# Weight sums on VectorE, squares on ScalarE, tiles of 512 bytes, seven products for four more chunks, and transposes of the identity at the start

## The chip, the cores and the metric

One core of a Trainium2 chip runs the whole program in one launch. The metric is the device time of one execution in microseconds (us). The kernel before takes 1533.81 us, the median of three runs (1532.96 to 1535.28).

## What is computed

Two layers of an encoder over 512 tokens of 1024 features, in float32. Each layer has three token mixers that share one input projection, gates, an output projection, a layer norm, and then the part that the change is about, a squared-ReLU network:

```python
ff = jnp.square(jax.nn.relu(x @ w_up[layer])) @ w_down[layer]      # (512,1024) @ (1024,4096), then @ (4096,1024)
x = layer_norm(DEEPNORM_ALPHA * x + ff, ln2_g[layer], ln2_b[layer])
```

## The kernel before, in words

**Products.** Every float32 operand is split into a high and a low part. ScalarE (ACT) writes the high part (L182 for weights, tiles `whi`), VectorE (DVE) subtracts it from the operand (L183, `wlo`), and `mm3` (L153 to L155) makes one product out of three matmuls of TensorE (PE): high by high, high by low, low by high. A weight chunk is 128 x 1024 numbers, 512 KB. `Stream` brings the chunks in a planned order: SyncE (SP) issues a load into one of two `raw` tiles, the chunk is split, and at most eight split chunks are held (five in one pool, three in another). One more chunk is split each time one is taken.

**The squared-ReLU network.** It runs in four quarters `q` of 8 chunks of 128 hidden features. For each chunk m, 24 matmuls make x @ w_up in a PSUM bank (`psu`). Then `hidden(m)` takes it over: ACT applies Relu into tile `f` (L910), DVE squares it in place (L911), ACT and DVE split it (`split_psum`, L231 and L232) into `hh` and `hl`. In quarters 0 to 2 DVE also makes sums of pairs of blocks (L918, L921). The tile `f` has one buffer. A pair of chunks (m even, m odd) shares it, so the Relu of the next pair waits until the last `hl` of this pair is written.

**Seven products.** In quarters 0 to 2 the 8 chunks of `w_down` are multiplied by the class `Fast`: two by two blocks, seven products instead of eight. Each product takes two split chunks (halves 0 and 1) and 24 matmuls into two `psd` banks, and DVE adds each bank to x (L259). The operands of the products are quarters of the weights and their differences: `operand(i, half)` gives seven operands for each half, four of which are a difference (L796, 128x1024, GpSimd = POOL). One load comes late: quarter 2 goes into the `y` tile (i = 5) only after i = 4 has been split from it, and the difference i = 6 needs it. All three `Fast` runs of a layer use the same raw tiles (`braw`). In quarter 3 the last 8 chunks go through `token_major` plainly: 8 chunks x 8 banks x 3 = 192 matmuls.

**Order.** Tile, the layer that places the instructions, orders each engine's queue. An engine takes its instructions strictly in that order, so an instruction that waits holds up all behind it. At the first quarter of a layer (q = 0) the first four chunks are done in two passes over the tokens, because the layer norm before it is still finishing.

**Tiles.** `LINE` = 16 numbers pads small tiles to 64 bytes, and the tile `edge` on the right side makes up for the rest.

Of the kernel before, what the change touches and what calls it, by code (L numbers as in the profile page):

```python
# [11 lines left out]
F32 = mybir.dt.float32  # L12
# [5 lines left out]
P = 128  # L18
L = 2
# [18 lines left out]
C_WID = 1280  # L38
LINE = 16


class Split:


    def __init__(self, hi, lo):
        self.hi, self.lo = hi, lo
# [82 lines left out]
def encoder(ctx: ExitStack, tc: tile.TileContext, x, x_t, w_qkv, w_c, w_gate, b_gate, qn, kn, rpb,  # L129
            w_ba, w_bb, w_bc, w_out, ln1_g, ln1_b, w_up, w_down, w_fast, ln2_g, ln2_b,  # L130
            mask_a, rope_a, rope_b, out):
# [5 lines left out]
    edge = ctx.enter_context(tc.tile_pool(name="edge", bufs=1, side="right"))  # L137
    edge.tile([P, LINE // 2], F32, name="edge")
    psum = ctx.enter_context(tc.tile_pool(name="psum", bufs=8, space=bass.MemoryType.PSUM))
# [9 lines left out]
    nhalf = const.tile([P, 16], F32, name="nhalf")  # L149
    nc.vector.memset(nhalf, -0.5)  # L150

    def mm3(ps, lhs, rhs, start, stop, again=False):
# [145 lines left out]
    def attention(l, keep, qk, open_heads):  # L298
# [72 lines left out]
        def norm_rotate(tb):  # L371
# [7 lines left out]
            yield 1  # L379
            ss = pool.tile([P, 2, LINE], F32, tag="ss", name="ss", bufs=2)[:, :, :10]  # L380
            nc.vector.tensor_reduce(ss[:, 0], sq, axis=AX.X, op=ALU.add)
# [128 lines left out]
        def scores(name, h, qb):  # L510
            ks, qs = pairs[name, h // 2]
            q, k = qs[h % 2], ks[h % 2]
            k0, k1 = keys_of(name, qb)
            n = (k1 - k0) * P
            ps = bank("pss")[:, :n]
            nc.tensor.matmul(ps, q[:, qb * P:(qb + 1) * P], k.hi[:, k0 * P:k1 * P], start=True, stop=False)
            nc.tensor.matmul(ps, q[:, qb * P:(qb + 1) * P], k.lo[:, k0 * P:k1 * P], start=False, stop=True)
            p = pool.tile([P, S], F32, tag="p", name="p", bufs=4)[:, :n]
            st = pool.tile([P, LINE], F32, tag="stat", name="stat", bufs=4)
# [132 lines left out]
        pool = open_heads()  # L652
        hb = keep.tile([P, 4 * KB], F32, tag="hb", name="hb")[:, :3 * KB]
        nc.sync.dma_start(hb, b_gate[l])
# [110 lines left out]
    class Fast:  # L765
# [8 lines left out]

        def __init__(self, pools, src):
            self.pools, self.src = pools, src
            self.b = {}

        def load(self, quarter, half, into):
            t = self.pools["mlp"].tile([P, 1024], F32, tag=f"b{into}{half}", name="braw")  # L780
            nc.sync.dma_start(t, self.src[quarter, half])
            self.b[into, half] = t

        def operand(self, i, half):

            if i == 0 and half == 0:
                for quarter in (0, 1, 3):
                    for h in range(2):
                        self.load(quarter, h, quarter)
            if i == 5:  # L790
                self.load(2, half, 1)
            b11, b12, b22 = (self.b[k, half] for k in (0, 1, 3))
            dst, a, b = ((b11, None, None), (b11, b12, b11), (b11, b22, b11), (b22, None, None),
                         (b12, b22, b12), (b12, None, None), (b11, b12, b11))[i]
            if a is not None:
                nc.gpsimd.tensor_tensor(dst, a, b, op=ALU.subtract)  # L796
            return dst

        def items(self):
            return [lambda i=i, half=half: self.operand(i, half) for i in range(7) for half in range(2)]  # L800

        def run(self, hid, done):
            ps = {}
            for a, _, name, (i, n) in self.ORDER:
                w = [stream.take(2) for _ in range(2)]
                new = name not in ps
                if new:
                    ps[name] = [bank("psd") for _ in range(2)]
                for t in range(2):
                    for j in range(4):  # L810
                        lhs = hid[j].map(lambda h: h[:, a - 1, t * P:(t + 1) * P])
                        mm3(ps[name][t], lhs, w[j // 2][:, j % 2], new and j == 0, j == 3, True)
                    done(2 * (1 - i) + t, n, ps[name][t])
# [23 lines left out]
    for l in range(L):  # L837
        with ExitStack() as left:
# [59 lines left out]
            for q in range(4):  # L898
                hid, sums = [], []

                def hidden(m, ps):
# [22 lines left out]
                for m0 in range(0, 8, 4):  # L924
                    cut = [(0, 2), (2, 4)] if q == 0 and m0 == 0 else [(0, 4)]
                    ws, ps = [], []
                    for a, b in cut:
                        for i in range(4):
# [8 lines left out]
                            elif i in (0, 2):  # L937
                                late.popleft()()

                if q < 3:  # L940
                    def add(tb, n, ps):
                        add_stats(mlp, xs[tb], ps, n, 1.0 if (tb, n) in started else ALPHA, None)
                        started.add((tb, n))

                    fast[q].run(sums, add)
                    continue
# [17 lines left out]
                stream.burst = 2  # L964
                whole = [h.map(lambda t: t[:, 2 * i:2 * i + 2].rearrange("p a n -> p (a n)")) for h in sums for i in range(2)]
                token_major(whole, 8, half_done, done, between)
                stream.burst = 1
# [56 lines left out]

def _quarters(w):

    w = w[:, :24 * P].reshape(L, 3, 2, 2, 2, P, 2, 512).transpose(0, 1, 4, 6, 2, 5, 3, 7)
    return w.reshape(L, 3, 4, 2, P, 1024)

# [52 lines left out]
```

## Time and profile before

| | |
|---|---|
| median of three runs | 1533.81 us |
| the profiled execution, all of it | 1538.57 us |
| its span, first to last instruction | 1536.8 us |
| PE busy | 1501.1 us, 98% |
| DVE busy | 1096.1 us, 71% |
| ACT busy | 688.0 us, 45% |
| POOL busy | 311.6 us, 20% |
| mean granted clock of TensorE | 0.991 |

Busy times are sums over the whole span; matmuls are pipelined, so a busy PE is not a PE at its peak. PE runs from 6.97 us almost to the end: where PE stands still, and at which clock it runs, is what the time is made of. [...]

### The profile page before, as it was taken

How to read it: one execution, taken by the hardware profiler on the slowest of the kernel's cores; microseconds unless marked ns; L12 is line 12 of the kernel's file. 1: busy time of each engine (PE TensorE's matmuls, PEld its weight loads, DVE VectorE, ACT ScalarE, POOL GpSimd, SP SyncE). 2: the span in 40 equal slices, each digit the busy share in tenths (PEclk: the TensorE clock that was granted, in tenths of full speed). 3: DMA queues.
4: the chain of work that ended last, by engine and by line, in shares of the span. 5: the costliest groups of instructions: out<-in, count | busy, mean ns of one | idle time of the engine just before them, and what ended most of it. 6: DMA issues, size and time to landing. Idle time of an engine off the chain costs nothing.

```text
span 1536.8 us, 19258 instructions
## 1 busy us (share of the span) xinstructions
PE 1501.1 (98%) x7256; PEld 1255.7 (82%) x7256; DVE 1096.1 (71%) x1722; ACT 688.0 (45%) x1096; POOL 311.6 (20%) x238
## 2 busy tenths in 40 slices
PE   7999999999998999999999999999999989999997
PEld 6888888888896888888888888888888968888886
DVE  4677977745588797964666787876447888979636
ACT  4565656533134343433236556565332343535320
POOL 0112212311142222210101141233111413222001
PEclk9999999999998999999999999999999999999999
DMA  6222321143242415042331323112441342340411
GB/s 218 84 79 70 112 68 53 58 164 118 75 178 81 139 56 164 1 131 85 114 129 56 99 77 110 55 55 76 160 133 56 152 137 83 91 129 28 138 55 55
DMA packets 43438, 150.63 MB, mean 98 GB/s; under 512 B 5073, under 2 KB 5713, under 8 KB 43345
## 3 DMA queue, kind: packets, MB, share of 16 engines
q1 hardware_dynamic: 43344, 149.40, 30.8%
q8 instruction: 57, 0.93, 0.2%
q14 instruction: 37, 0.30, 0.1%
HBM read 145.19 MB, written 4.19 MB: 97 GB/s over the span
## 4 chain that ended last, share of the span: by engine, by line
PE 88%; DVE 7%; ACT 2%; issue 1%; DMA 1%; POOL 0%; SPq 0%; POOLq 0%; DVEq 0%; ACTq 0%
PE psd L153 8%; PE psd L154 8%; PE psd L155 8%; PE psu L154 6%; PE psu L153 6%; PE psu L155 6%; PE psg L155 6%; PE psg L154 6%; PE psg L153 6%; PE psp L547 3%; PE psq L153 2%; PE psq L155 2%; PE psq L154 2%; DVE wlo L183 2%; PE psb L155 2%; PE psb L153 2%
## 5 line engine op out<-in xcount | busy, mean ns | idle before, releaser
L183 DVE TENSOR_TENSOR wlo<-raw,whi 128x1024 fp32r<-128x1024 f32 (+1 forms) x198 | 247.9, 1253 | 204.2 <-ACT whi L182 201.9
L182 ACT ACTIVATE whi<-raw 128x1024 fp32r<-128x1024 f32 (+1 forms) x198 | 207.7, 1051 | 268.7 <-DMA raw<-in_w_up 110.6
L153 PE MATMUL psu<-xTh,whi 128*128 128x512 f32 (+1 forms) x576 | 210.8, 366 | 0.0
L154 PE MATMUL psu<-xTl,whi 128*128 128x512 f32 (+1 forms) x576 | 210.7, 366 | 0.0
L155 PE MATMUL psu<-xTh,wlo 128*128 128x512 f32 (+1 forms) x576 | 210.4, 365 | 0.0
L153 PE MATMUL psd<-whi,hh 128*128 128x512 f32 x464 | 183.2, 395 | 14.8 <-ACT hh L231 14.8
L796 POOL TENSOR_TENSOR braw<-braw 128x1024 f32<-128x1024 f32 x48 | 130.1, 2713 | 332.7 <-DVE wlo L183 169.2
L154 PE MATMUL psd<-wlo,hh 128*128 128x512 f32 x464 | 182.3, 393 | 0.0
L155 PE MATMUL psd<-whi,hl 128*128 128x512 f32 x464 | 182.2, 393 | 0.0
L153 PE MATMUL psg<-xTh,whi 128*128 128x512 f32 x384 | 156.7, 408 | 0.0
L155 PE MATMUL psg<-xTh,wlo 128*128 128x512 f32 x384 | 151.6, 395 | 0.0
L154 PE MATMUL psg<-xTl,whi 128*128 128x512 f32 x384 | 151.5, 395 | 0.0
L532 POOL TENSOR_SCALAR p<-p,stat 128x512 f32<-128x512 f32 x96 | 70.4, 734 | 361.5 <-DVE stat L531 247.1
L183 DVE TENSOR_TENSOR wlo<-braw,whi 128x1024 fp32r<-128x1024 f32 x84 | 126.7, 1508 | 18.3 <-ACT whi L182 16.7
L231 ACT ACTIVATE hh<-f 128x768 fp32r<-128x768 f32 (+2 forms) x88 | 60.8, 691 | 144.8 <-DVE f L918 79.4
L153 PEld LDWEIGHTS psu<-xTh,whi 128*128 128x128 f32 x576 | 108.6, 189 | 17.5
L154 PEld LDWEIGHTS psu<-xTl,whi 128*128 128x128 f32 x576 | 108.6, 189 | 17.5
L155 PEld LDWEIGHTS psu<-xTh,wlo 128*128 128x128 f32 x576 | 108.6, 189 | 17.5
L153 PEld LDWEIGHTS psd<-whi,hh 128*128 128x128 f32 x464 | 88.3, 190 | 34.8 <-ACT hh L231 16.5
L182 ACT ACTIVATE whi<-braw 128x1024 fp32r<-128x1024 f32 x84 | 87.9, 1051 | 47.9 <-DMA braw<-in_w_fast 25.3
L155 PEld LDWEIGHTS psd<-whi,hl 128*128 128x128 f32 x464 | 88.1, 190 | 18.9 <-DVE hl L232 0.5
L154 PEld LDWEIGHTS psd<-wlo,hh 128*128 128x128 f32 x464 | 88.3, 190 | 18.3
(121 smaller groups left out, 2991.3 us busy)
## 6 DMA issues: line engine op xcount, KB each, us to landing
raw<-in_w_up SPq DMA_DIRECT2D x64, 512.0 KB, 3.7
raw<-in_w_gate SPq DMA_DIRECT2D x48, 512.0 KB, 3.6
braw<-in_w_fast SPq DMA_DIRECT2D x48, 512.0 KB, 3.7
raw<-in_w_qkv SPq DMA_DIRECT2D x22, 512.0 KB, 3.6
raw<-in_w_out SPq DMA_DIRECT2D x16, 512.0 KB, 3.5
raw<-in_w_down SPq DMA_DIRECT2D x16, 512.0 KB, 3.5
raw<-in_w_c SPq DMA_DIRECT2D x12, 512.0 KB, 3.6
bias<-in_rpb SPq DMA_DIRECT2D x8, 640.0 KB, 4.0
```

Source lines behind the costliest of these rows:

```text
L153: nc.tensor.matmul(ps, lhs.hi, rhs.hi, start=start, stop=False, skip_group_check=again)
L154: nc.tensor.matmul(ps, lhs.hi, rhs.lo, start=False, stop=False, skip_group_check=again)
L155: nc.tensor.matmul(ps, lhs.lo, rhs.hi, start=False, stop=stop, skip_group_check=again)
L182: nc.scalar.activation(hi[:, s], raw[:, s], AF.Copy)
L183: nc.vector.tensor_tensor(lo[:, s], raw[:, s], f32(hi[:, s]), op=ALU.subtract)
L231: nc.scalar.activation(dst.hi, ps, AF.Copy)
L532: (nc.vector if name == "c" else nc.gpsimd).tensor_scalar(p, p, st[:, 3:4], 1.0, op0=ALU.mult, op1=ALU.mult)
L547: nc.tensor.transpose(ps[:, j * P:(j + 1) * P], p[:, j * P:(j + 1) * P], ident)
L796: nc.gpsimd.tensor_tensor(dst, a, b, op=ALU.subtract)
```

## The change

Five things change. (1) The differences of weights (L796) go from POOL to DVE. (2) The square (L911) goes from DVE to ACT (`AF.Square`). (3) All tiles are padded so that they start at multiples of 512 bytes: `ROW` = 128 numbers in place of `LINE` in most small tiles, a tile `pad`, another `edge`. (4) In quarter 3, chunks 0 to 3 go through `Fast` with one half (`tiles` = 1): seven products of 12 matmuls, in place of 4 chunks x 24; chunks 4 to 7 go through `token_major` as before. For this `Fast`, quarter 2 of the weights has a tile of its own (`y1`) and the first difference another (`x1`). (5) 24 transposes of the identity into an unused bank stand ahead of PE's first matmul.

```diff
+    const.tile([P, 3 * ROW // 4], F32, name="pad")
     ident = const.tile([P, P], F32, name="ident")
     make_identity(nc, ident)
...
+    idle = bank("idle")
+    for _ in range(24):
+        nc.tensor.transpose(idle[:, :P], ident, ident)
...
         def operand(self, i, half):
+            one = self.tiles == 1
             if i == 0 and half == 0:
...
+                if one:
+                    self.b["y1"], self.b["x1"] = self.room("y1"), self.room("x1")
+                    nc.sync.dma_start(self.b["y1"], self.src[2, 0])
+            if i == 5 and not one:
+                self.load(2, f"y{half}")
+            x, y, w = (self.b[f"{name}{half}"] for name in "xyw")
+            t1, last, b21 = (self.b["x1"], self.b["x1"], self.b["y1"]) if one else (x, x, y)
+            dst, a, b = ((x, None, None), (t1, y, x), (x, w, t1), (w, None, None),
+                         (y, w, y), (b21, None, None), (last, b21, x))[i]
             if a is not None:
-                nc.gpsimd.tensor_tensor(dst, a, b, op=ALU.subtract)
+                nc.vector.tensor_tensor(dst, a, b, op=ALU.subtract)
...
-                w = [stream.take(2) for _ in range(2)]
+                w = [stream.take(2) for _ in range(self.tiles)]
...
-                    for j in range(4):
+                    for j in range(2 * self.tiles):
...
-            fast = [Fast(pools, w_fast[l, q]) for q in range(3)]
+            fast = [Fast(pools, w_fast[l, q], 2) for q in range(3)] + [Fast(pools, w_last[l], 1)]
             plan = []
             for q in range(4):
                 plan += [w_up[l, q * 8 + m] for m in range(8)]
-                plan += fast[q].items() if q < 3 else [w_down[l, m] for m in range(8)]
+                plan += fast[q].items()
+            plan += [w_down[l, m] for m in range(4)]
...
                     nc.scalar.activation(r, ps.rearrange("p (a n) -> p a n", a=2), AF.Relu)
-                    nc.vector.tensor_tensor(r, r, r, op=ALU.mult)
-                    if q == 3:
+                    nc.scalar.activation(r, r, AF.Square)
+                    if q == 3 and m > 3:
...
-                token_major(whole, 8, half_done, done, between)
+                token_major(whole, 4, half_done, done, between)
```

On DVE in quarter 0 of layer 0, before, from the last `wlo` of the up-projection on (`f` 128x512 is a square, `f` 128x256 a sum of blocks, `wlo<-braw` the split of a `Fast` operand):

```order
L183 TENSOR_TENSOR wlo<-raw,whi 128x1024
L911 TENSOR_TENSOR f<-f 128x512
L921 TENSOR_TENSOR f<-f 128x256
L183 TENSOR_TENSOR wlo<-braw,whi 128x1024
L232 TENSOR_TENSOR hl<-f,hh 128x256
L183 TENSOR_TENSOR wlo<-braw,whi 128x1024
L911 TENSOR_TENSOR f<-f 128x512
L918 TENSOR_TENSOR f<-f 128x256
L921 TENSOR_TENSOR f<-f 128x256 x2
L183 TENSOR_TENSOR wlo<-braw,whi 128x1024
L232 TENSOR_TENSOR hl<-f,hh 128x768 x2
L183 TENSOR_TENSOR wlo<-braw,whi 128x1024
```

The same place now:

```order
L190 TENSOR_TENSOR wlo<-raw,whi 128x1024
L190 TENSOR_TENSOR wlo<-braw,whi 128x1024
L239 TENSOR_TENSOR hl<-f,hh 128x256
L937 TENSOR_TENSOR f<-f 128x256
L811 TENSOR_TENSOR braw<-braw 128x1024
L190 TENSOR_TENSOR wlo<-braw,whi 128x1024
L934 TENSOR_TENSOR f<-f 128x256
L811 TENSOR_TENSOR braw<-braw 128x1024
L937 TENSOR_TENSOR f<-f 128x256
L239 TENSOR_TENSOR hl<-f,hh 128x768
L937 TENSOR_TENSOR f<-f 128x256
L190 TENSOR_TENSOR wlo<-braw,whi 128x1024 x2
```

The squares have left DVE's queue here, and the differences (`braw<-braw`) stand between the splits and the sums of blocks; six of them stand ahead of the `hl` on which the first product of this quarter waits.

On DVE a little later, when the first products of that quarter run (`x<-x,psd` takes a finished bank), before:

```order
L259 SCALAR_TENSOR_TENSOR x<-x,psd 128x512
L183 TENSOR_TENSOR wlo<-braw,whi 128x1024
L259 SCALAR_TENSOR_TENSOR x<-x,psd 128x512
L183 TENSOR_TENSOR wlo<-braw,whi 128x1024
L259 SCALAR_TENSOR_TENSOR x<-x,psd 128x512
```

And now:

```order
L266 SCALAR_TENSOR_TENSOR x<-x,psd 128x512
L190 TENSOR_TENSOR wlo<-braw,whi 128x1024
L266 SCALAR_TENSOR_TENSOR x<-x,psd 128x512
L811 TENSOR_TENSOR braw<-braw 128x1024
L190 TENSOR_TENSOR wlo<-braw,whi 128x1024
L266 SCALAR_TENSOR_TENSOR x<-x,psd 128x512
L811 TENSOR_TENSOR braw<-braw 128x1024
L266 SCALAR_TENSOR_TENSOR x<-x,psd 128x512
```

The two differences i = 6 of the run, which need the late load of quarter 2, now stand in DVE's queue between the takings of the banks.

On ACT in quarter 0 of layer 0, now, from the last up-projection chunk on (`f<-psu` is the Relu; `f<-f` is the square, which was on DVE; before, the rows are the same without `f<-f`):

```order
L189 ACTIVATE whi<-raw 128x1024
L926 ACTIVATE f<-psu 128x512
L189 ACTIVATE whi<-braw 128x1024
L927 ACTIVATE f<-f 128x512
L238 ACTIVATE hh<-f 128x256
L189 ACTIVATE whi<-braw 128x1024
L926 ACTIVATE f<-psu 128x512
L927 ACTIVATE f<-f 128x512
```

The square now follows the Relu on the same engine, and the split follows the square.

## Rows read from the trace of the kernel before

**Rows 1.** The page, part 1: busy us, share of the span, instructions.

```profile
PE 1501.1 (98%) x7256; PEld 1255.7 (82%) x7256; DVE 1096.1 (71%) x1722; ACT 688.0 (45%) x1096; POOL 311.6 (20%) x238
```

**Rows 2.** Waits of PE: who waited for whom, us in total, times, longest.

```profile
PE psd L153 <- ACT hh L231: 14.8, 3, 7.4
...
PE psp L547 <- POOL p L532: 4.6, 2, 2.5
```

**Rows 3.** Windows of PE: stretch, length, busy (instructions), granted clock, DMA share, GB/s.

```profile
520.00:560.00 40.00, 40.00 (x179) 1.00 0.12 37
565.00:600.00 35.00, 35.00 (x156) 1.00 0.56 172
...
54.90:59.00 4.10, 4.10 (x15) 0.58 0.27 109
475.20:485.30 10.10, 5.69 (x13) 0.50 0.35 105
1236.40:1243.10 6.70, 3.83 (x9) 0.50 0.36 94
...
6.90:17.40 10.50, 9.28 (x19) 1.00 0.77 294
```

**Rows 4.** Timeline of PE at quarter 0: start us, us, what [idle before].

```profile
470.56 0.39 PE L154 MATMUL psd<-wlo,hh 128*128 128x512 f32 x1
...
472.15 0.39 PE L155 MATMUL psd<-whi,hl 128*128 128x512 f32 x1
479.61 0.80 PE L153 MATMUL psd<-whi,hh 128*128 128x512 f32 x1 [7.07 <-ACT hh L231]
...
1239.27 0.80 PE L153 MATMUL psd<-whi,hh 128*128 128x512 f32 x1 [7.36 <-ACT hh L231]
```

**Rows 5.** Timeline of DVE in quarter 0 of layer 0.

```profile
444.01 2.71 DVE L183 TENSOR_TENSOR wlo<-braw,whi 128x1024 fp32r<-128x1024 f32 x1 [0.65 <-ACT whi L182]
...
461.20 3.49 DVE L911 TENSOR_TENSOR f<-f 128x512 f32<-128x512 f32 x2
...
464.95 0.41 DVE L918 TENSOR_TENSOR f<-f 128x256 f32<-128x256 f32 x1
...
468.41 0.95 DVE L232 TENSOR_TENSOR hl<-f,hh 128x768 fp32r<-128x768 f32 x1
470.09 0.69 DVE L911 TENSOR_TENSOR f<-f 128x512 f32<-128x512 f32 x1 [0.72 <-ACT f L910]
...
479.59 0.43 DVE L232 TENSOR_TENSOR hl<-f,hh 128x256 fp32r<-128x256 f32 x1
```

**Rows 6.** Groups by line and shape: busy us, mean ns of one, idle before.

```profile
L183 DVE TENSOR_TENSOR wlo<-raw,whi 128x1024 fp32r<-128x1024 f32 x11 | 13.4, 1221 | 10.2 <-ACT whi L182 10.1
L183 DVE TENSOR_TENSOR wlo<-braw,whi 128x1024 fp32r<-128x1024 f32 x84 | 126.7, 1508 | 18.3 <-ACT whi L182 16.7 <-DMA raw<-in_w_up 0.5 <-PE psu L154 0.5
L231 ACT ACTIVATE hh<-f 128x512 fp32r<-128x512 f32 x16 | 10.1, 633 | 19.9 <-DVE f L911 19.9
L376 ACT ACTIVATE sq<-rw 128x640 f32<-128x640 f32 x8 | 5.9, 740 | 0.3
```

**Rows 7.** Window of quarter 0, layer 0: PE, PEld, DVE, ACT, POOL busy (instructions), clock, DMA.

```profile
439.40:470.30 30.90, 30.90 (x174) 27.18 (x173) 29.24 (x25) 11.74 (x16) 16.74 (x6) 1.00 0.25 99
```

**Rows 8.** Timeline: the identity on POOL, PE's first operands, transposes at the slow clock.

```profile
1.00 0.29 POOL masks.py:199 TENSOR_SCALAR_AFFINE_SELECT ident<-ident 128x128 f32<-128x128 f32 x1
...
11.30 0.79 PE L153 MATMUL psq<-whi,xTh 128*128 128x512 f32 x1 [1.11 <-ACT xTh L825]
...
813.52 1.11 PE L547 MATMUL psp<-ident,p 128*128 128x128 f32 x4 [2.51 <-POOL p L532]
814.28 0.78 PE L154 MATMUL psg<-xTl,whi 128*128 128x512 f32 x1
```

**Rows 9.** The late load: POOL's waits for it, and its time from issue to landing.

```profile
POOL braw L796 <- DMA braw<-in_w_fast: 162.8, 11, 25.8
...
braw<-in_w_fast SPq DMA_DIRECT2D x48, 512.0 KB, 3.7
```

More of the change, by code (lines that the diff above doesn't have):

```diff
@@ L39 @@
 LINE = 16
+ROW = 128
 class Split:
@@ L137, in encoder @@
     edge = ctx.enter_context(tc.tile_pool(name="edge", bufs=1, side="right"))
-    edge.tile([P, LINE // 2], F32, name="edge")
+    edge.tile([P, ROW - LINE // 2], F32, name="edge")
     psum = ctx.enter_context(tc.tile_pool(name="psum", bufs=8, space=bass.MemoryType.PSUM))
@@ L145, in f32 @@
         return ap.bitcast(F32)
+    const.tile([P, 3 * ROW // 4], F32, name="pad")
     ident = const.tile([P, P], F32, name="ident")
     make_identity(nc, ident)
-    nhalf = const.tile([P, 16], F32, name="nhalf")
+    nhalf = const.tile([P, ROW], F32, name="nhalf")[:, :16]
     nc.vector.memset(nhalf, -0.5)
+    idle = bank("idle")
+    for _ in range(24):
+        nc.tensor.transpose(idle[:, :P], ident, ident)
     def mm3(ps, lhs, rhs, start, stop, again=False):
@@ L379, in norm_rotate @@
             yield 1
-            ss = pool.tile([P, 2, LINE], F32, tag="ss", name="ss", bufs=2)[:, :, :10]
+            ss = pool.tile([P, 2, ROW // 2], F32, tag="ss", name="ss", bufs=2)[:, :, :10]
             nc.vector.tensor_reduce(ss[:, 0], sq, axis=AX.X, op=ALU.add)
@@ L518, in scores @@
             p = pool.tile([P, S], F32, tag="p", name="p", bufs=4)[:, :n]
-            st = pool.tile([P, LINE], F32, tag="stat", name="stat", bufs=4)
+            st = pool.tile([P, ROW], F32, tag="stat", name="stat", bufs=4)
             if name == "b":
@@ L652, in attention @@
         pool = open_heads()
-        hb = keep.tile([P, 4 * KB], F32, tag="hb", name="hb")[:, :3 * KB]
+        hb = keep.tile([P, ROW], F32, tag="hb", name="hb")[:, :3 * KB]
         nc.sync.dma_start(hb, b_gate[l])
@@ L773, in encoder, with __init__, room @@
                  (6, 4, "x", (1, 1)), (3, 5, "y", (0, 0)), (2, 6, "x", (1, 0)))
-        def __init__(self, pools, src):
-            self.pools, self.src = pools, src
+        def __init__(self, pools, src, tiles):
+            self.pools, self.src, self.tiles = pools, src, tiles
             self.b = {}
[L779 to L782, printed above, removed]
+        def room(self, name):
+            return self.pools["mlp"].tile([P, 1024], F32, tag=f"b{name}", name="braw")
@@ L784, in operand, with load @@
+        def load(self, quarter, name):
+            self.b[name] = t = self.room(name)
+            nc.sync.dma_start(t, self.src[quarter, int(name[1])])
         def operand(self, i, half):
+            one = self.tiles == 1
             if i == 0 and half == 0:
[L787 to L792, printed above, removed]
@@ L793, in operand @@
-            dst, a, b = ((b11, None, None), (b11, b12, b11), (b11, b22, b11), (b22, None, None),
-                         (b12, b22, b12), (b12, None, None), (b11, b12, b11))[i]
+                for name, quarter in (("x", 0), ("y", 1), ("w", 3)):
+                    for h in range(self.tiles):
+                        self.load(quarter, f"{name}{h}")
+                if one:
+                    self.b["y1"], self.b["x1"] = self.room("y1"), self.room("x1")
+                    nc.sync.dma_start(self.b["y1"], self.src[2, 0])
@@ L797, in operand @@
             return dst
         def items(self):
-            return [lambda i=i, half=half: self.operand(i, half) for i in range(7) for half in range(2)]
+            return [lambda i=i, half=half: self.operand(i, half) for i in range(7) for half in range(self.tiles)]
         def run(self, hid, done):
@@ L938, in encoder, with add @@
                                 late.popleft()()
+                def add(tb, n, ps):
+                    add_stats(mlp, xs[tb], ps, n, 1.0 if (tb, n) in started else ALPHA, None)
+                    started.add((tb, n))
+                fast[q].run(sums, add)
                 if q < 3:
[L941 to L945, printed above, removed]
                     continue
@@ L964, in encoder @@
                 stream.burst = 2
-                whole = [h.map(lambda t: t[:, 2 * i:2 * i + 2].rearrange("p a n -> p (a n)")) for h in sums for i in range(2)]
-                token_major(whole, 8, half_done, done, between)
+                whole = [h.map(lambda t: t[:, 2 * i:2 * i + 2].rearrange("p a n -> p (a n)")) for h in sums[2:] for i in range(2)]
+                token_major(whole, 4, half_done, done, between)
                 stream.burst = 1
@@ L1022, in _by_rows, with _quarters @@
     return w.reshape(k // P // per, per, P, n).transpose(0, 2, 1, 3).reshape(-1, P, 1024)
[L1025 to L1028 removed]
+def _quarters(w, groups, tiles):
+    w = w.reshape(L, groups, tiles, 2, 2, P, 2, 512).transpose(0, 1, 4, 6, 2, 5, 3, 7)
+    return w.reshape(L, groups, 4, tiles, P, 1024)
 def _swap(g):
```

9 lines of the change are left out of this document (5 added, 4 removed).

## The prediction

> **What bounds the kernel now.** I read the busy times first, then PE's own waits, then its clock by stretch, and only then the engines that PE waits for. PE is busy 98% of the span [rows 1], and what PE waits for adds up to little: 14.8 us for `hh` and 4.6 us for `p` [rows 2], beside its start. Where nothing waits, its matmuls stand 0.227 us apart: eight of them from 470.56 to 472.15 us, 1.59 us over seven steps [rows 4]. The long stretches of up-projection (520 to 560 us) and of seven products (565 to 600 us) run at that pace, 4.5 matmuls a microsecond in both [rows 3], and nearly all else does. So the time is the number of matmuls by 0.227 us, plus the places where PE stands or runs at the slow clock. Work on DVE, ACT and POOL counts only where it makes PE stand.
>
> There are two such places of weight, and they are the same place of the program in either layer: the first product of quarter 0. In layer 0 PE makes nine matmuls of it, then stands 7.07 us until 479.61 us for the split of chunk 6; in layer 1 it stands 7.36 us until 1239.27 us [rows 4]. [...] The two places together cost 7.07 + 2.6 + 7.36 + 1.8 = 18.8 us; with the third, small wait in [rows 2] (14.8 - 14.4 = 0.4 us) it is 19.2 us.
>
> Why does PE stand there? DVE is busy 29.24 of the 30.9 us ahead of the stop, ACT only 11.74 [rows 7]. Six of DVE's rows there, from 444.01 to 461.20 us (the first and the last stand in [rows 5]), are far longer than the same work elsewhere: two weight splits, a sum of blocks, and a pair each of sums, of 768-wide splits and of squares take 19.12 us together. Clean, a weight split takes 1.22 us [rows 6], a sum 0.41, a 768-wide split 0.95, a square 0.69 [rows 5], and the six would take 2.44 + 0.41 + 0.82 + 1.90 + 1.38 = 6.95 us. POOL makes six differences at the same time (16.74 us busy [rows 7]): 12.2 us go to the two engines holding each other up.
>
> **The change, part by part.**
>
> *Fewer matmuls.* In quarter 3, 4 chunks x 24 = 96 matmuls become 7 x 12 = 84. Two layers: 24 fewer, 24 x 0.227 = **5.4 us**, all on PE. The price is three more weight splits a layer, 1.22 us each on DVE [rows 6] and about as much on ACT, and four differences. Under the seven short products (84 x 0.227 = 19 us) DVE takes 14 banks over, at 0.69 us for 512 columns [rows 5], and makes four splits: 14.5 us, it fits. Their operands are split during the up-projection, and no late load stands in this run, since quarter 2 has its own tile. I take nothing for it; were the cover gone, DVE would lag by a microsecond or so a layer.
>
> *Differences to DVE, squares to ACT.* A difference does not occur on DVE. The nearest rows are the split with the same shape: 1.22 us clean, 1.51 us in the mean of those with POOL often beside them [rows 6]. POOL now has nothing to do in these stretches, so I take 1.22. A square of a 128x512 tile does not occur on ACT: 0.63 us for a copy of that size, 0.74 us for a square of 640 columns [rows 6]; I take 0.65. ACT gets 64 of them, 42 us, in stretches where it is busy under half the time [rows 7]: hidden. For DVE's queue up to the `hl` of chunk 6, which ended at 480.02 us [rows 5]: the 12.2 us of holding up go, seven squares go (7 x 0.69 = 4.8), six differences come (7.3). That is 9.7 us less, so that `hl` is there at 470.3 us. PE wants it with its tenth matmul of the product, at 472.4 us, so the stop is gone with 2 us to spare; in layer 1, where the stop is 0.3 us longer, the same sum leaves 1.7 us. What is late next is chunk 7, whose rows the second product wants 5.4 us later; Relu, square, sum, split high and low (0.63 + 0.65 + 0.41 + 0.9, an estimate for 768 columns on ACT, + 0.95) are 3.5 us behind its bank, so it fits. Gain taken: **19.2 us**. Bounds: 0 (the stops stay) and 19.2.
>
> *Transposes of the identity.* The identity is ready at 1.29 us [rows 8]. Four transposes at the slow clock take 814.28 - 813.52 = 0.76 us [rows 8], about 0.2 each, so 24 end near 6.3 us, ahead of PE's first operands, which come after 6.90 us [rows 3]: no cost. At its start PE runs 19 matmuls in 9.28 us of busy time [rows 3], 0.43 us apart like the stretches at 0.50, though the clock column reads 1.00 there. Were the clock up by then, at most 19 x 0.2 = 3.8 us were to be had. Against that: the operands come piecemeal, and PE still stands before 11.30 us for `xTh` [rows 8]; a stop of 2.5 us for `p` is followed by a stretch with a mean clock of 0.58 [rows 2, 3]. Bounds 0 and 3.8; I take **1 us**, nearer the lower end for that reason.
> [...] No run here shows PE with transposes alone. [...]
>
> *Tiles of 512 bytes.* No row shows a tile that starts otherwise. The matmul's pace is the same with a moving operand in one piece of 2 KB (weights, 565 to 600 us) and in four pieces of 512 bytes (`xTh`, 520 to 560 us) [rows 3]; if crossing a boundary cost something, four pieces would cost more. I take 0. [...]
>
> **Sum.** 5.4 + 19.2 + 1 = 25.6 us. Against the profiled execution's own 1538.57 us that gives 1513.0. That execution lies 4.8 us above the median of 1533.81; the difference may be of the kind that goes (slow clock behind the stops) or of another, so I place the result between 1513.0 and 1508.2: **1510 us**.
>
> **Rivals.**
> *The start address does set the pace.* [...] For it: the pace is the one thing that bounds the whole program. Against it: the equal pace of the two kinds of operand above.
> [...]
>
> *The stop shrinks but stays.* The spare 2 us are gone if the six differences and eight splits cost 0.15 us more each, or if the chain over the single `f` buffer, which goes from ACT to DVE and back twice a pair, waits at a hop more. [...]
>
> *The stops stay whole*, because the order on ACT decides and not DVE's load: only 5.4 us and the start are gained, 1527 us. Against it: ACT is busy 11.74 of 30.9 us [rows 7].
>
> *Slower: DVE waits for the late load.* The differences i = 6 now stand in DVE's queue between the takings of the banks (see the order above). They need quarter 2, whose load is issued only after the split of i = 4 and takes 3.7 us to land; on POOL the same differences waited 162.8 us in all, up to 25.8 us at a time [rows 9]. A DVE that waits there takes no bank and splits nothing. A product takes 5.4 us and its bank is written again two products later, so PE feels the wait once it is over about 4 us. From a stop of 4.4 us in each of the six runs the gain of 25.6 us is used up; with a wait of a load's whole 3.7 us beyond the slack, and ten matmuls at the slow clock behind it (2 us), it is 6 x 5.7 = 34 us: 1544 us. Against it: by then the splits of i = 4 are two products ahead of PE, and the wait I count at DVE's head is about 2 us.
>
> **How the numbers follow.** Forecast (1510): 0.66. Stop shrinks (1520): 0.14. Stops stay (1527): 0.08. Slower (1540 and more): 0.06. Pace rises (1425 to 1450): 0.06. The range of 1500 to 1524 us holds the first two with the bounds of the start (0 to 3.8) and of the 4.8 us, and some room below for a slightly higher pace in the attention part; it leaves out 0.20. Faster by over 0.2% (which is about what a measurement of this kernel can tell) means under 1530.7 us: 0.66 + 0.14 + 0.06 and most of the 0.08, 0.92. Within 0.2%: 0.03, the weakest form of the stops that stay or a short wait for the load. Slower: 0.05.
>
> **What would show it.** In the profile after: PE with no wait for `hh` over 1 us near 472 and 1230 us and no stretch at 0.50 there; DVE's splits and sums near 1.22 and 0.42 us in the quarters; POOL idle in them; 7256 - 24 + 24 = 7256 matmuls, the first 24 transposes; the pace still 0.227 us. I would be wrong if the pace changes, if PE waits for `psd` banks or for `wlo` inside the products (DVE at the head of its queue waiting for a load), or if the stop at quarter 0 only moves to the next chunk.

## The result, and the profile after

The changed kernel takes 1507.31 us (median; 1506.78 to 1509.10), the kernel before, run beside it, 1534.55 us: ratio 0.9823, 95% interval 0.9805 to 0.984, so 27 us or 1.8% faster. The forecast was 1510 us, with a range of 1500 to 1524. The profiled execution took 1506.91 us, against 1538.57 us before. The two traces stand 31.7 us apart, the medians 27: the profiled execution of before was one of its longer ones, that of after was not.

The page of the changed kernel, parts 1 and 4 (busy us, share of the span, instructions; then the shares of the chain that ended last), answers [rows 1]:

```profile
PE 1488.2 (99%) x7256; PEld 1250.8 (83%) x7256; DVE 1059.8 (70%) x1768; ACT 738.5 (49%) x1170; POOL 181.9 (12%) x190
...
PE 95%; DVE 2%; DMA 1%; ACT 1%; issue 1%; POOL 0%; SPq 0%; POOLq 0%; DVEq 0%; ACTq 0%
```

PE has as many instructions as before (24 matmuls fewer, 24 transposes more) and is busy 12.9 us less. POOL's work fell from 311.6 to 181.9 us. DVE took over 56 differences (68.0 us, below) and gave 64 squares away (48 us at 0.75 before), 20 us more by that sum, and is busy 36 us *less*. What PE still waits for, against [rows 2] (who waited for whom, us in total, times, longest):

```profile
PE psp L554 <- POOL p L539: 4.3, 2, 2.4
PE psq L160 <- ACT xTh L840: 2.0, 1, 2.0
PE idle L157 <- POOL ident masks.py:199: 1.3, 1, 1.3
```

The waits for `hh` are gone, all three. The wait for `p` stands as it was. The groups of DVE and ACT by line and shape (busy us, mean ns of one | idle before) answer [rows 6]:

```profile
L190 DVE TENSOR_TENSOR wlo<-braw,whi 128x1024 fp32r<-128x1024 f32 x98 | 119.5, 1223 | 71.9 <-ACT whi L189 71.7
L811 DVE TENSOR_TENSOR braw<-braw 128x1024 f32<-128x1024 f32 x56 | 68.0, 1219 | 8.7 <-DMA braw<-in_w_fast 4.2 <-issue 2.3 <-DMA braw<-in_w_last 2.3
L937 DVE TENSOR_TENSOR f<-f 128x256 f32<-128x256 f32 x84 | 35.1, 422 | 3.3 <-ACT f L927 2.4
L927 ACT ACTIVATE f<-f 128x512 f32<-128x512 f32 x64 | 40.3, 633 | 1.8
```

A difference on DVE takes 1.22 us and a square on ACT 0.63 us. The splits of `braw` fell from 1.51 to 1.22 us in the mean. DVE stood only 6.5 us in the whole run for the loads of its differences. PE at quarter 0 of layer 0, and the split that it stood for before (PE's and DVE's timelines), answer [rows 4] and [rows 5]:

```profile
464.95 0.42 DVE L239 TENSOR_TENSOR hl<-f,hh 128x256 fp32r<-128x256 f32 x1
...
468.46 0.39 PE L162 MATMUL psd<-whi,hl 128*128 128x512 f32 x1
468.69 0.39 PE L160 MATMUL psd<-whi,hh 128*128 128x512 f32 x1
468.92 0.39 PE L161 MATMUL psd<-wlo,hh 128*128 128x512 f32 x1
```

The matmul of 468.69 us is the one that began at 479.61 us before, behind a stop of 7.07 us. Now nothing stands ahead of it, and the split is over 3.3 us before it. Windows of PE (length, busy (instructions), granted clock, DMA share, GB/s) answer [rows 3]:

```profile
520.00:560.00 40.00, 40.00 (x178) 1.00 0.18 51
565.00:600.00 35.00, 35.00 (x156) 1.00 0.52 165
440.00:480.00 40.00, 40.00 (x197) 1.00 0.26 86
11.60:14.90 3.30, 3.26 (x8) 0.50 0.83 325
52.50:55.90 3.40, 3.40 (x11) 0.50 0.51 154
796.60:800.00 3.40, 3.12 (x10) 0.50 0.56 161
```

The two long stretches run at the old pace (156 matmuls in 35 us, as before). Quarter 0 now runs through at 1.00. Slow stretches (granted clock 0.50) are left behind the stop at the start and behind the two stops for `p`. In such a stretch of before two neighbours of one product stand 0.43 us apart:

```profile
480.20 0.63 PE L154 MATMUL psd<-wlo,hh 128*128 128x512 f32 x1
480.63 0.63 PE L155 MATMUL psd<-whi,hl 128*128 128x512 f32 x1
```

From 480.20 to 484.89 us eleven steps take 4.69 us, 0.427 each, where 0.227 is the pace at 1.00.

Where the trace's 31.7 us come from can be read by pairing the same matmul in both traces:

| the same matmul | before, us | after, us | lead | gained in the stretch |
|---|---|---|---|---|
| project, first layer, early | 17.42 | 15.80 | 1.6 | 1.6: the start |
| gate, behind the stop for `p` | 58.77 | 56.85 | 1.9 | 0.3 |
| first of the output projection | 379.08 | 375.38 | 3.7 | 1.8: attention, little by little |
| quarter 0, behind the slow stretch | 485.32 | 471.63 | 13.7 | 10.0: stop and slow clock |
| last of quarter 3, layer 0 | 728.0 | 711.45 | 16.55 | 2.7 for 12 matmuls, 0.15 |
| attention of layer 1, late | 1128.33 | 1109.99 | 18.35 | 1.8: little by little |
| quarter 0, layer 1 | 1243.22 | 1215.31 | 27.9 | 9.5: stop and slow clock |
| last matmul | 1528.25 | 1496.6 | 31.65 | 2.7 for 12 matmuls, 1.0 |

The 1.6 us of the start cannot be put down to the transposes. Four kernels without them (b_act, b_tiles, a_noidle and b_dve below) had the matmul of 17.42 us 1.3, 1.6, 1.4 and 2.7 us earlier than this execution of before: before was late there.

### The profile page after: what moved, and what is told of

Same layout as the page of the kernel before. It is cut to its first block, busy times and chain, and to the rows that moved or that the text cites. A ratio compares the mean times of both kernels' runs of the same rounds, so it can differ in the third digit from the quotient of the medians.

```text
span 1505.1 us, 19285 instructions
## 1 busy us (share of the span) xinstructions
PE 1488.2 (99%) x7256; PEld 1250.8 (83%) x7256; DVE 1059.8 (70%) x1768; ACT 738.5 (49%) x1170; POOL 181.9 (12%) x190
## 3 DMA queue, kind: packets, MB, share of 16 engines
q1 hardware_dynamic: 43344, 149.40, 31.5%
## 4 chain that ended last, share of the span: by engine, by line
PE 95%; DVE 2%; DMA 1%; ACT 1%; issue 1%; POOL 0%; SPq 0%; POOLq 0%; DVEq 0%; ACTq 0%
PE psd L161 8%; PE psd L162 8%; PE psd L160 8%; PE psu L161 8%; PE psu L162 8%; PE psu L160 8%; PE psg L162 6%; PE psg L161 6%; PE psg L160 6%; PE psp L554 3%; PE psq L162 2%; PE psq L160 2%; PE psq L161 2%; PE psb L160 2%; PE psb L161 2%; PE psb L162 2%
## 5 line engine op out<-in xcount | busy, mean ns | idle before, releaser
L190 DVE TENSOR_TENSOR wlo<-raw,whi 128x1024 fp32r<-128x1024 f32 (+1 forms) x190 | 237.5, 1250 | 157.5 <-ACT whi L189 154.2
L189 ACT ACTIVATE whi<-raw 128x1024 fp32r<-128x1024 f32 (+1 forms) x190 | 199.0, 1051 | 253.6 <-DMA raw<-in_w_up 115.7
L160 PE MATMUL psd<-whi,hh 128*128 128x512 f32 x456 | 177.6, 389 | 0.0
L162 PE MATMUL psd<-whi,hl 128*128 128x512 f32 x456 | 177.4, 389 | 0.0
L161 PE MATMUL psd<-wlo,hh 128*128 128x512 f32 x456 | 177.4, 389 | 0.0
L190 DVE TENSOR_TENSOR wlo<-braw,whi 128x1024 fp32r<-128x1024 f32 x98 | 119.5, 1223 | 71.9 <-ACT whi L189 71.7
L189 ACT ACTIVATE whi<-braw 128x1024 fp32r<-128x1024 f32 x98 | 103.7, 1058 | 115.4 <-PE psu L161 73.0
L276 POOL TENSOR_TENSOR ve<-ve,nhalf 128x1 f32<-128x1 f32 x16 | 24.1, 1508 | 738.9 <-DVE ve L275 738.9
L266 DVE SCALAR_TENSOR_TENSOR x<-x,psd 128x512 f32<-128x512 f32 x144 | 97.0, 681 | 18.4 <-PE psd L162 17.9
```

Source lines behind the costliest of these rows:

```text
L160: nc.tensor.matmul(ps, lhs.hi, rhs.hi, start=start, stop=False, skip_group_check=again)
L161: nc.tensor.matmul(ps, lhs.hi, rhs.lo, start=False, stop=False, skip_group_check=again)
L162: nc.tensor.matmul(ps, lhs.lo, rhs.hi, start=False, stop=stop, skip_group_check=again)
L189: nc.scalar.activation(hi[:, s], raw[:, s], AF.Copy)
L190: nc.vector.tensor_tensor(lo[:, s], raw[:, s], f32(hi[:, s]), op=ALU.subtract)
L266: nc.vector.scalar_tensor_tensor(z[:, s], z[:, s], scale, ps, op0=ALU.mult, op1=ALU.add)
```

## The experiments

All times are medians. The kernel before took 1534.6 to 1536.1 us beside them, so medians from different series can differ by over 1 us without any change of the kernel; the ratio in brackets is to the kernel before of the same series, with its 95% interval. Kernels named a are the changed one with one thing undone or added, kernels named b are the one before with one part of the change alone.

### Which of the two moves ends the stops

Differences on DVE alone, before with one line:

```diff
-                nc.gpsimd.tensor_tensor(dst, a, b, op=ALU.subtract)
+                nc.vector.tensor_tensor(dst, a, b, op=ALU.subtract)
```

> The kernel before with one part of the change alone: the weight differences on VectorE instead of GpSimd. Theory (the sum of VectorE's queue: 12.2 us of holding up go, six differences of 1.22 us = 7.3 us come): the split of chunk 6 is 4.9 us earlier, PE's stop at quarter 0 shrinks from 7.1 to about 2.2 us a layer and the slow clock behind it stays; 10 us gained, about 1524.5 us. Rival 1 (GpSimd beside VectorE is the whole cause): both stops and their slow clock gone, 19 us gained, about 1515.5 us. Rival 2 (the squares' place on VectorE is the whole cause): no gain, about 1534 us. A wait of VectorE for the late load would make it slower than 1534.5 us.

Measured: **1513.67 us** (ratio 0.9862, 0.9845 to 0.9878). PE has no wait for `hh` at all.

Squares on ACT alone:

```diff
-                    nc.vector.tensor_tensor(r, r, r, op=ALU.mult)
+                    nc.scalar.activation(r, r, AF.Square)
```

> The kernel before with one part of the change alone: the squares on ScalarE instead of VectorE. Theory (sum of VectorE's queue): seven squares of 0.69 us = 4.8 us go, and of the holding up by GpSimd the 2.1 us that two pairs of squares had (3.49 against 1.38 us) may go too: the stop shrinks from 7.1 to between 0.2 and 2.3 us a layer, 10 to 14 us gained, 1520 to 1524.5 us. Rival 1 (GpSimd beside VectorE is the whole cause): stops stay, about 1534 us. Rival 2 (the squares are the whole cause): both stops and their slow clock gone, about 1515.5 us.

Measured: **1525.02 us** (0.9933, 0.9917 to 0.9949). PE's waits in it:

```profile
PE psd L153 <- ACT hh L231: 6.3, 2, 3.2
```

The changed kernel with the differences back on POOL (the first diff, turned round):

> The changed kernel with one part undone: the weight differences back on GpSimd. In the changed kernel hh of chunk 6 is ready at 464.92 us and wanted at 468.69 us, 3.8 us to spare. Theory (sum of VectorE's queue): 7.3 us of differences go, 10.1 us of holding up come back (12.2 less the squares' 2.1), 2.8 us later, inside the spare 3.8 us: no stop or one under 1 us a layer, 1507 to 1512 us. Rival 1 (GpSimd beside VectorE is the whole cause): both stops back, about 1526 us. Rival 2 (squares alone): 1507 us.

Measured: **1517.61 us** (0.9886, 0.9873 to 0.99).

The changed kernel with the squares back on DVE (the second diff, turned round):

> The changed kernel with one part undone: the squares back on VectorE. Theory (sum of VectorE's queue): seven squares of 0.69 us make the split of chunk 6 4.8 us later, 1.0 us more than the spare 3.8 us: a stop of about 1 us a layer with perhaps ten matmuls at the slow clock (2 us) behind it, 1509 to 1513 us. Rival 1 (GpSimd beside VectorE is the whole cause): no stop, 1507 us. Rival 2 (the squares are the whole cause): both stops back, about 1526 us.

Measured: **1506.55 us** (0.9812, 0.9799 to 0.9826).

| kernel | differences | squares | stop, us a layer | us |
|---|---|---|---|---|
| before | POOL | DVE | 7.1, 7.4 | 1534.55 |
| b_act | POOL | ACT | 3.2 | 1525.02 |
| b_dve | DVE | DVE | none | 1513.67 |
| a_pool | POOL | ACT | 3.1 | 1517.61 |
| a_dvesq | DVE | DVE | none | 1506.55 |
| after | DVE | ACT | none | 1507.31 |

The differences end the stops; the squares alone halve them, and beside the differences they bring nothing that can be measured. Rival 1 of the expectations (GpSimd beside VectorE is the whole cause) fits the two kernels with all differences on DVE, b_dve and a_dvesq. It doesn't fit b_act, where it had no gain and 11 us were gained, nor a_pool, which lies between the theory and this rival. What counts is the whole of DVE's queue, as the theory had it, with another split of the holding up, and the rows of a_pool show which. Quarter 0 in the changed kernel with the differences on POOL, POOL's timeline and DVE's:

```profile
440.77 2.53 POOL L811 TENSOR_TENSOR braw<-braw 128x1024 f32<-128x1024 f32 x1 [12.53 <-DVE wlo L190]
444.80 7.62 POOL L811 TENSOR_TENSOR braw<-braw 128x1024 f32<-128x1024 f32 x3 [1.50 <-DVE wlo L190]
454.44 3.05 POOL L811 TENSOR_TENSOR braw<-braw 128x1024 f32<-128x1024 f32 x1 [2.03 <-DVE wlo L190]
458.66 2.52 POOL L811 TENSOR_TENSOR braw<-braw 128x1024 f32<-128x1024 f32 x1 [1.17 <-DVE wlo L190]
```

```profile
440.94 2.64 DVE L937 TENSOR_TENSOR f<-f 128x256 f32<-128x256 f32 x1
...
445.08 5.06 DVE L937 TENSOR_TENSOR f<-f 128x256 f32<-128x256 f32 x2
450.07 3.16 DVE L239 TENSOR_TENSOR hl<-f,hh 128x768 fp32r<-128x768 f32 x1
...
455.16 3.42 DVE L190 TENSOR_TENSOR wlo<-braw,whi 128x1024 fp32r<-128x1024 f32 x1
...
458.84 2.62 DVE L934 TENSOR_TENSOR f<-f 128x256 f32<-128x256 f32 x1
```

Each of POOL's six differences holds one row of DVE up, whichever stands beside it, and here always by the same: 2.64 - 0.42 = 2.2 us for a block of 256, 3.16 - 0.95 = 2.2 for a split of 768, 3.42 - 1.22 = 2.2 for a weight split. In all 13.1 us. (In the kernel before it was 2.1 to 2.2 us for five of the six and 1.5 for one.) So a difference on POOL costs DVE about 2.2 us; done by DVE itself it costs 1.22. That is why DVE's busy time falls when it takes work over: 1097.8 us in this kernel, 1059.8 in after with the 68.0 us of differences among them. Over the whole run that is (1097.8 - 1059.8 + 68.0) / 56 = 1.9 us a difference. In those six rows it is 2.2 us of the 2.5 that a single difference takes on POOL; what makes the one wait for the other isn't shown. The same rows also correct the expectation for this kernel: the 2.1 us that stood on the squares' row before were not theirs, they fall on another row once the squares have left. With 13.1 instead of 10.1 us the split is 13.1 - 7.3 = 5.8 us later, 2.0 us beyond the spare 3.8. A stop of 3.1 was measured. The rest is in the trace: counted from the same weight split, `hh` of the chunk is ready 36.0 us behind it here and 29.5 in after, 6.5 us later and not 5.8, and PE comes to the place 0.6 us earlier.

With the differences alone on DVE, the split came earlier than the sum said. Counted from the last weight split of the up-projection's own stream, it ended 40.6 us behind it before (439.40 to 480.02) and 33.6 us behind it in b_dve (436.61 to 470.24): 7.0 us earlier, where the sum had 4.9. Part of the rest are DVE's own waits at its queue's head, which fell from 1.9 us (0.65 + 0.72 + 0.53, for `whi` and `f`) to 0.75 (0.18 + 0.57). There the split is only just in time: `hh` of the chunk is ready at 468.95 us and PE's matmul on it starts at 469.65 us; the one on `hl`, ready at 470.24, starts at 470.33, behind the next block's. The squares' move to ACT turned the 0.7 us for `hh` into 3.8, and such a reserve shows in no time.

### The tiles

The changed kernel with the paddings back at 64 bytes, and the kernel before with 512-byte tiles alone; the core of the edit (the second has it turned round):

```diff
-ROW = 128
-    const.tile([P, 3 * ROW // 4], F32, name="pad")
-            st = pool.tile([P, ROW], F32, tag="stat", name="stat", bufs=4)
+            st = pool.tile([P, LINE], F32, tag="stat", name="stat", bufs=4)
```

> The changed kernel with one part undone: all paddings back to 64 bytes, so that the large tiles again start 64 bytes past a 128-byte multiple. Between the two traces the same matmuls drift 1.8 us apart from 60 to 379 us and 2.0 us in the same part of layer 1, with the differences on VectorE alone they do not. Theory (the 512-byte start gives those 3.8 us in the attention part): 1511 us, and the up-projection and seven products at the same 0.227 us. Rival 1 (it is the order of the engines' work, not the address): 1507 us. Rival 2 (the address sets the pace everywhere, some ns of each of 7256 matmuls): over 1515 us.

> The kernel before with one part of the change alone: the 512-byte tiles. Theory (3.8 us in the attention part): about 1531 us, stops at quarter 0 unchanged (7.1 and 7.4 us). Rival 1 (no effect of the address): 1535 us. Rival 2 (address sets the pace everywhere): under 1527 us.

Measured: **1511.91 us** without them (0.9845, 0.9831 to 0.9858), **1532.29 us** with them alone (0.9976, 0.9967 to 0.9986): 4.6 us and 3.8 us, both as the theory had it. The branch matmuls (`psb`) of before, of after, without the tiles and with them alone (count, duration ns min/median/max):

```profile
L153 PE MATMUL psb<-oh,whi x128: 388/395/483, 203.0 to 1137.0; 128*128 128x512 f32 x128
```

```profile
L160 PE MATMUL psb<-oh,whi x128: 389/389/481, 200.6 to 1118.6; 128*128 128x512 f32 x128
```

```profile
L158 PE MATMUL psb<-oh,whi x128: 388/395/482, 203.2 to 1124.6; 128*128 128x512 f32 x128
```

```profile
L155 PE MATMUL psb<-oh,whi x128: 389/389/481, 200.8 to 1132.0; 128*128 128x512 f32 x128
```

The median is 395 ns with 64-byte paddings and 389 with 512, in either kernel. The durations contain the pipeline; from start to start the median of these is 0.234 and 0.227 us. The gate matmuls (`psg`) go from 0.231 to 0.227 in the same way. In the mean it is less, since part of the matmuls are as slow in either: about 4 ns for the 384 branch matmuls and 1 ns for the 1152 gate matmuls, 2.8 us together, against 3.6 us that the attention parts of the two layers gave in the table above. Up-projection and seven products have 0.227 us in all four.

Is it where the large tiles start? The next kernel keeps the small tiles' 512-byte distance, but puts everything 64 bytes behind a 512-byte multiple:

```diff
-    edge.tile([P, ROW - LINE // 2], F32, name="edge")
-    const.tile([P, 3 * ROW // 4], F32, name="pad")
+    edge.tile([P, 2 * ROW - LINE // 2 - LINE], F32, name="edge")
+    const.tile([P, 3 * ROW // 4 + LINE], F32, name="pad")
```

> The changed kernel with one thing changed: every tile stands 64 bytes behind a 512-byte multiple (the first tile of either side 64 bytes longer), while the small tiles keep their 512-byte distance. Theory (the start of the large tiles decides): the attention part is slower as with 64-byte paddings, medians of gate matmuls 0.230 us and more instead of 0.227, 1511 us. Rival (the distance of the small tiles decides): 1507 us.

Measured: **1506.77 us** (0.9817, 0.9804 to 0.983), and:

```profile
L160 PE MATMUL psb<-oh,whi x128: 389/389/481, 202.2 to 1120.4; 128*128 128x512 f32 x128
```

So a start at a 512-byte multiple isn't needed; the theory fell. Two things still go together: the small tiles are 512 bytes apart, and all large tiles keep one common offset to a 512-byte multiple (with 64-byte paddings they lie at 64, 192, 320 or 448 by the sizes of the tiles in the program). Which of the two does it was not tried.

### Fewer matmuls

Quarter 3 again in plain products:

```diff
-                plan += fast[q].items()
-            plan += [w_down[l, m] for m in range(4)]
+                plan += fast[q].items() if q < 3 else [w_down[l, m] for m in range(8)]
-                token_major(whole, 4, half_done, done, between)
+                token_major(whole, 8, half_done, done, between)
```

> The changed kernel with one part undone: quarter 3 again with eight chunks in plain products, 96 matmuls a layer instead of 84. Theory (all on PE, nothing hidden, nothing lost beside it): 24 x 0.227 = 5.4 us more, 1512.5 us. Rival (the seven products cost PE something at their start or end): less than 4 us more, under 1511 us.

Measured: **1512.84 us** (0.9854, 0.9841 to 0.9868), 5.5 us more than the changed kernel beside it. 24 x 0.227 = 5.4: nothing is hidden or lost that the medians, whose runs lie 2.6 and 3.6 us apart, can tell.

### The transposes, and the clock

Without the 24 transposes, and the changed kernel once more:

```diff
-    idle = bank("idle")
-    for _ in range(24):
-        nc.tensor.transpose(idle[:, :P], ident, ident)
```

> The changed kernel with one part undone: without the 24 transposes at the start. In the changed kernel the granted clock rose at 4.72 us, during the transposes, and the project's matmul that ran at 17.42 us before the change ran 1.6 us earlier after it. Theory (the transposes raise the clock and that is worth the 1.6 us): 1509 us. [...]

> The changed kernel once more, beside the three below on the same chip. 1506.5 to 1508.5 us. If the 24 transposes at the start were worth their 1.6 us, it is 1.5 us and more under the kernel without them (1506.45 us); if not, it is the same within 1 us.

Measured: **1506.45 us** without them (0.981, 0.9797 to 0.9823), **1507.34 us** with them (0.9822, 0.9808 to 0.9835), 1507.31 the first time. They bring nothing that can be measured. But they do raise the clock. In after the transposes themselves stand 0.213 us apart up to 4.60 us and 0.109 from 4.77 us on. The same matmuls of the start, with them and without (PE's timelines):

```profile
7.50 0.40 PE L160 MATMUL psq<-whi,xTh 128*128 128x512 f32 x1
7.73 0.44 PE L161 MATMUL psq<-wlo,xTh 128*128 128x512 f32 x1
8.01 0.40 PE L162 MATMUL psq<-whi,xTl 128*128 128x512 f32 x1
10.38 0.50 PE L160 MATMUL psq<-whi,xTh 128*128 128x512 f32 x1 [1.98 <-ACT xTh L840]
```

```profile
8.15 0.63 PE L155 MATMUL psq<-whi,xTh 128*128 128x512 f32 x1
8.58 0.63 PE L156 MATMUL psq<-wlo,xTh 128*128 128x512 f32 x1
9.01 0.63 PE L157 MATMUL psq<-whi,xTl 128*128 128x512 f32 x1
10.62 0.80 PE L155 MATMUL psq<-whi,xTh 128*128 128x512 f32 x1 [0.98 <-ACT xTh L835]
```

Behind transposes alone they follow each other by 0.23 to 0.28 us, near the pace at a granted clock of 1.00 (0.227), without them by 0.43, the pace at 0.50 (0.427). So transposes alone had brought the clock up here.

Why is nothing gained? The executions with transposes are of two kinds: PE's waits for `p` add up to 4.1 to 4.8 us in four of them and to 6.9 to 7.0 in the other three. In the four (after, the same kernel once more, a_dvesq, a_plain) the clock falls again at the stops for the next operands. In after the seventh matmul waits for `xTh` and begins at 10.38 us, without transposes at 10.62; behind that stop the clock is at 0.50 (11.6 to 14.9 us), and 0.2 us of lead are left.

In the other three (a_pool, a_lines, a_shift) no slow stretch came at 11 us, and ACT took the same bank of the project over (`rw<-psq`) at 32.44, 32.94 and 32.27 us, 33.46 in after. There PE reached the stop for `p` early, and stood there longer: 4.5 to 4.6 us instead of 2.0 (after) and 2.2 (without transposes). It went on at 53.58, 54.21 and 53.67 us, but at 52.12 in after and at 52.57 without any transposes. The longest waits of PE in a_lines, and of ACT ahead of that stop (20 to 50 us) in a_lines and in after:

```profile
PE psp L552 <- POOL p L537: 7.0, 2, 4.6
```

```profile
ACT whi L187 <- DMA raw<-in_w_gate: 3.9, 1, 3.9
```

```profile
ACT whi L189 <- DMA raw<-in_w_gate: 1.3, 1, 1.3
```

ACT stands for a weight load ahead of the work on the first `p`. That load was late for a reason of its own, which DVE's timeline shows, in a_lines and in after:

```profile
31.47 0.42 DVE L383 TENSOR_TENSOR cs<-gqk,ropeb 128x256 f32<-128x256 f32 x1 [6.27 <-DMA gqk<-in_kn]
```

```profile
28.73 0.43 DVE L385 TENSOR_TENSOR cs<-gqk,ropeb 128x256 f32<-128x256 f32 x1 [3.91 <-DMA gqk<-in_kn]
```

In these three executions alone SP's issue of the first small `gqk` load took 1.2 to 1.8 us (0.4 in the other eleven profiled ones), and DVE stood for that tile at the head of its queue until 30.9 to 31.5 us (28.4 to 29.7 in the others). The weight splits behind it, the gate load that needs their `raw` tile, and `p` came later. An early start doesn't bring this with it: in b_dve and in the kernel with bridges below PE was as early (at its stop for `p` at 49.2 us in b_dve, 50.1 in after), the load was in time, and the first `p` came at 51.40 and 51.07 us. So in the three executions a late load ate the gain of the start; why its issue took longer isn't shown.

If transposes bring the clock up, they can hold it up in the other stops too. Sixteen behind the first six matmuls, and sixteen ahead of the first transposes of `p` in either layer:

```diff
+            if (name, h, qb) == ("a", 0, 0):
+                for _ in range(16):
+                    nc.tensor.transpose(ps[:, :P], ident, ident)
             for j in range(n):
                 nc.tensor.transpose(ps[:, j * P:(j + 1) * P], p[:, j * P:(j + 1) * P], ident)
...
+                if l == 0 and before and step == 1:
+                    for _ in range(16):
+                        nc.tensor.transpose(idle[:, :P], ident, ident)
```

> The changed kernel with more of one part: 16 more transposes of the identity in three places where PE stands while it has no operands: behind the first six matmuls at the start (stop of 2.4 us), and ahead of the first transposes of p in either layer (stops of 2.0 to 2.5 us). 16 at 0.109 us are 1.75 us, shorter than each stop. Theory (transposes keep the clock up): no slow stretch behind the three stops, 3 x 1.7 us less, about 1502 us. [...] Rival 2 (the transposes delay the work behind them): 1507 to 1511 us.

Measured: **1504.88 us** (0.9799, 0.9785 to 0.9812; from 1504.64 to 1505.09). Windows of PE in it, at the start and around both stops for `p`:

```profile
12.00:17.00 5.00, 5.00 (x22) 1.00 0.52 192
47.80:56.00 8.20, 6.88 (x43) 1.00 0.42 128
790.00:800.00 10.00, 8.26 (x50) 1.00 0.35 105
```

No slow stretch is left but the one behind the last matmul; the mean granted clock is 0.999 (0.995 in after). 2.4 us are won by the medians, not the 5.1 expected. Paired with after, matmul by matmul, its lead is 1.2 us behind the start, 0.1 behind the first stop for `p`, 1.6 behind the stretch that was slow there, 0.7 behind the second stop and 1.8 at the end: the clock gave 1.2 + 1.5 + 1.1 = 3.8 us, and each stop for `p` took about 1 us back. The timelines show by what: the 16 transposes and those of `p` stand four gate matmuls further ahead in PE's queue, so four matmuls (0.9 us) that filled time ahead of the stop in after stand behind it here. Nor is every such stop of the changed kernel followed by a slow stretch: one of 2.4 us, until 797 us, was (after), one of 2.6 us at the same place was not (without transposes, mean granted clock 0.997). The runs of the kernel with bridges lie within 0.5 us, those of the changed kernel within 3.6; that the slow stretches are the variable part fits with this, and isn't shown.

Last, beside this, the first block of `p` of either layer normalized on DVE:

```diff
-                (nc.vector if name == "c" else nc.gpsimd).tensor_scalar(p, p, st[:, 3:4], 1.0, op0=ALU.mult, op1=ALU.mult)
+                (nc.vector if name == "c" or (name, h, qb) == ("a", 0, 0) else nc.gpsimd).tensor_scalar(p, p, st[:, 3:4], 1.0, op0=ALU.mult, op1=ALU.mult)
```

> The changed kernel with 48 more transposes in the three stops (1504.9 us) and, beside it, the first block of p of either layer normalized on VectorE instead of GpSimd (three blocks stand in one row of GpSimd there: 3.05 us for three, 1.0 us each, and PE goes on 1.7 us after that row's start). Theory (the chain to the first p sets when PE goes on): the stops of 1.3 and 1.7 us shrink by about 1 us each, 1503 us. Rival (VectorE's queue is late by as much, or the next block is late): 1505 us.

Measured: **1502.75 us** (0.979, 0.9776 to 0.9803), 4.6 us under the changed kernel and the fastest here. PE's wait for `p`:

```profile
PE psp L560 <- DVE p L542: 0.6, 2, 0.5
```

It was 3.1 us with the bridges alone; 2.1 us gained, as expected (the two medians are of different series; the wait that is gone, 2.5 us, is of one size with it).

## Why the prediction was right, and where it was not

- **What bounds the kernel** (matmuls by 0.227 us, and the places where PE stands): right. The stops of quarter 0 and their slow clock gave 10.0 + 9.5 = 19.5 us in the trace, 19.2 were forecast. In those 19.2, 2.6 and 1.8 us stand for the 13 and 9 matmuls at a granted clock of 0.50 [rows 3], 0.427 us apart instead of 0.227. The changed kernel has no stop for `hh`; a_pool has one of 3.1 us a layer and takes 1517.61 us.
- **Why PE stands there** (DVE held up by POOL): right in kind, and shown by b_dve and a_pool. The step that failed is to split the holding up by rows, as if it went with them. It goes by POOL's differences, about 2.2 us each, and moves to other rows when the squares have left. "Seven squares go" (4.8 us) was needed in the sum to reach the end of the stop, but b_dve ends it without them, since 7.0 us went where the two terms of the differences gave 4.9. The total for `hl` of chunk 6 (9.7 us earlier) was near: from the same weight split it came at 30.0 us (435.38 to 465.37) instead of 40.6, 10.6 us earlier.
- **Prices of the moved work:** 1.22 us for a difference (as taken), 0.63 for a square on ACT (0.65), no wait for chunk 7.
- **Late load:** DVE stood 6.5 us in all for it, spread over the quarters; PE felt nothing. That rival didn't come.
- **Fewer matmuls:** 5.4 forecast, 5.5 measured.
- **Transposes:** 1 us forecast within 0 to 3.8, nothing measured. The doubt was right in part (the operands come piecemeal, and the clock falls again at the stops); that a late load would eat the gain in other executions was not foreseen.
- **Tiles of 512 bytes:** 0 forecast, 3.8 to 4.6 us measured. This is the largest error of the sum. No run shows the 1425 to 1450 us of a pace that rises everywhere: up-projection and seven products stay at 0.227 us. The argument from pieces of 2 KB and 512 bytes did not bear on it. I compared the pace in two stretches, up-projection and seven products, and wrote that "nearly all else" runs so. The attention part did not: 0.231 to 0.234 us for gates and branches stood in the trace of before. I never grouped the matmuls there by their spacing.
- **From the profiled execution to the median:** the sum was 25.6 us against the trace, and 1510 us is 23.8 under the median, so 1.8 us were counted for the profile's being long. Measured were 31.7 us against the trace and 27.2 between medians, 4.5 us. So the gain in the trace was 6.1 us larger than the sum (3.6 of it in the attention parts), and the way to the median took 2.7 of that back: that the forecast is only 2.7 us off is in part luck.

The parts alone add up to more than the whole: 22.4 (differences, from 1536.1) + 5.5 + 4.2 = 32 us, against 27 to 29. In the profiled execution of b_dve no slow stretch followed the second stop for `p` (1.7 us; mean granted clock 0.997), and its first `p` came 0.7 us earlier than in after. So part of the surplus is of the kind that also comes and goes between runs of one kernel; that this is all of it isn't shown.

## What to carry to other kernels

Where DVE's rows are of very uneven length (here a sum of blocks took 0.42 or 2.64 us), lay POOL's timeline beside them: a POOL instruction can cost DVE more time than the work itself would (here 2.2 us against 1.22), and then taking the work over *lowers* DVE's load (here from 1097.8 to 1059.8 us). Look for the pace of matmuls group by group, in every stage, before an edit to addresses is priced at nothing. A gain ahead of a stop that another chain ends (here loads, then `p`) lasts only as far as that chain comes earlier too, so price an edit to a start by the first wait behind it, and look at several executions of it: here the same start came out in two ways.

## What the hardware showed that I had not expected

- A POOL difference of 128x1024 (2.5 to 3.05 us) held a DVE row beside it up by 2.2 us, the same for rows of 0.42, 0.95 and 1.22 us (a_pool); by 1.9 us in the mean of the run.
- Paddings of 64 instead of 512 bytes between small tiles cost branches about 4 ns a matmul in the mean and gates 1 (7 and 4 ns in the medians), and up-projection and seven products nothing (0.227 us in all four kernels). A common offset of 64 bytes cost nothing that shows (a_shift 1506.77 us, the changed kernel 1507.34 beside it).
- Transposes of the identity alone were enough to bring the granted clock up (at 4.72 us in after, before any other matmul: 0.213 us a transpose ahead of it, 0.109 behind it) and to hold it at 1.00 over three stops (the kernel with bridges). Of two stops of like length (2.4 and 2.6 us) at one place the shorter was followed by a granted clock of 0.50 (after, 796.6 to 800.0 us), the longer was not (without transposes).
